# Another buffer pool for the last tile of a gated feed-forward result

## The chip, the cores and the metric

The kernel runs on one core of a Trainium2 chip. Its time is the device time of one launch, in microseconds (us); lower is better. Before the change it took 1318.67 us, the median of three runs (1316.35 to 1319.25). In what follows PE is the matrix engine, PEld its weight loads, DVE the vector engine, ACT the scalar engine, POOL the general engine, and SP the engine that issues most of the DMA transfers.

## The reference

Two layers work on 512 tokens of width 1024 in float32. Layer 0 mixes tokens by latent attention, layer 1 by a gated linear recurrence. Behind the mixer each layer does the same three steps:

```python
x = layer_norm(DEEPNORM_ALPHA * x + h, ln_mix_g[i], ln_mix_b[i])
x = layer_norm(DEEPNORM_ALPHA * x + swiglu_ffn(x, ffn_w_in[i], ffn_w_down[i]), ln_ffn_g[i], ln_ffn_b[i])
x = x + jax.nn.sigmoid(x @ ple_w_gate[i]) * (p[i] @ ple_w_proj[i])

def swiglu_ffn(x, w_in, w_down):
    h = x @ w_in
    g, u = h[..., :D_FF], h[..., D_FF:]
    return (jax.nn.silu(g) * u) @ w_down
```

The change lies in `swiglu_ffn`, once in each layer. D_FF is 2816, which is 22 blocks of 128.

## The kernel before, in words

**Number format.** A float32 product is made of three matmuls on split operands: each operand is a rounded high part and a low part (what is left), and `mm3` (lines 197 to 202) issues high x high, high x low and low x high. So every operand is split first: ACT copies the high part (line 179) and DVE subtracts it to get the low part (line 180). For weights of gate/up that come from memory, `split_dma` (lines 182 to 186) leaves the subtraction to a transfer: ACT writes the high part (184) and its negative (185), and POOL issues a transfer that adds the raw weights onto it (186).

**Gate/up** (`gate_up`, lines 380 to 476). One block j makes 128 columns of silu(g)·u for all 512 tokens. Blocks 0 and 1 are done plainly; blocks 2 to 21 use a Winograd scheme with seven products instead of eight. A product is four slices of the contraction, three matmuls each: 12 matmuls, so 84 per block. `prep(j)` loads the two weight blocks (SP, lines 391 and 392), forms the sums `ta` and `tb` on DVE (398 to 401), and splits: `h1`, `l1` and the pair `b22` with the help of POOL's transfers (395, 403), `h2`, `l2` from `ta` (405) and `h3`, `l3` from `tb` (407). `block(j)` then runs the products in the order A11·B11, A12·B21, S1·T1, S2·T2, A22·T4, S4·B22, S3·T3, and evacuates them with copies on ACT (439) and sums on DVE (446, 459 to 465). `b22` is first read by the sixth product, `h3` and `l3` by the fourth.

**The result** is kept in tiles of four blocks (`out`, lines 417 to 422). Five tiles of 8 KB per partition hold blocks 0 to 19; the last two blocks, 20 and 21, get a tile of 4 KB, [128, 2, 512] float32.

**The down projection** (`ffn`, lines 478 to 508) takes the 22 blocks one after the other. For each, SP loads 512 KB of down weights into a `raw` buffer, which are split into `whi` and `wlo` (`unit`, 188 to 195); `hsplit` (485 to 488) splits the block's result into a 4 KB `ma` tile; PE does 24 matmuls into eight banks.

**Buffers.** `mid` (171) hands out 4 KB buffers of two kinds, `ma` and `mb`, five of each (line 49). In gate/up each block takes three `ma` (`ta`, `tb`, `b22`) and two `mb` (`h3`, `l3`). There are five `whi`, five `wlo` and three `raw` buffers.

**The order.** A scheduler at compile time puts the instructions of each engine into one fixed queue, by the program's order and by when it expects operands and a free buffer. A tile whose buffer is not free there has its instructions put further back. On the chip each engine runs its queue strictly in order.

Of the kernel before, what the change touches and what calls it, by code (L numbers as in the profile page):

```python
# [29 lines left out]
P = 128  # L30
S = 512
# [114 lines left out]
class Builder:  # L146
# [233 lines left out]
    def gate_up(self, l, xT):  # L380
# [5 lines left out]
        hT = []  # L386
# [30 lines left out]
        def out(j):  # L417
            if j < 20 and j % 4 == 0:
                hT.append(self.slot([P, 4, S]))
            elif j == 20:  # L420
                hT.append(self.mid([P, 2, S]))
            return hT[j // 4][:, j % 4]

        def plain(h, w, half):
# [10 lines left out]
        def block(j):  # L435
            w = prep(j)
            h = out(j)
            part = lambda: self.small([P, N], tag="part", bufs=7)
            copy = lambda dst, src: nc.scalar.activation(dst, src[:, :N], AF.Copy)  # L439
# [26 lines left out]


        hs = [out(j) for j in range(2)]
        ws = [[self.unit(win[j, q], True) for q in range(2)] for j in range(2)]
        for half in range(2):  # L470
# [503 lines left out]
```

## Time and profile before

| | |
|---|---|
| time, median of 3 | 1318.67 us |
| profiled execution, its own time | 1319.56 us |
| its span, first to last instruction | 1317.8 us |
| PE busy | 1278.0 us (97%) |
| DVE busy | 813.1 us (62%) |
| ACT busy | 656.8 us (50%) |
| mean granted TensorE clock | 0.993 |

A span is measured between the first and the last instruction; the time of the execution includes the 1.76 us around it. PE is the engine with the least idle time, so the question is where PE waits, and on whom. The granted clock is the share of full speed at which PE was allowed to run. Tile names in the profile are those of the program without their numbers, so `ma` is any tile from the `ma` buffers.

### The profile page before, as it was taken

What the parts mean: (1) busy time and instruction counts of PE and PEld (TensorE: products, weight loads), DVE (VectorE), ACT (ScalarE), POOL (GpSimd) and SP (SyncE); (2) the same over time, 40 slices, a digit from 0 to 9 for tenths busy, and PEclk for the clock granted to TensorE, in tenths of its full rate; (3) what the DMA queues carried; (4) which work ended last, traced back from release to release, by engine and by line L of the source; (5) the groups of instructions that cost most, each with busy time, mean ns of one, the idle gap of its engine ahead of it and who ended that gap; (6) DMA issues with size and microseconds to landing.
All of it is one profiled execution on the core that took longest, in us unless ns stands there. A gap on an engine that the chain in (4) does not pass through costs nothing.

```text
span 1317.8 us, 20055 instructions
## 1 busy us (share of the span) xinstructions
PE 1278.0 (97%) x7900; PEld 1138.5 (86%) x7900; DVE 813.1 (62%) x1452; ACT 656.8 (50%) x1140; POOL 154.8 (12%) x167
## 2 busy tenths in 40 slices
PE   8999999999997999999999999999999999899998
PEld 8787889999997888888888887888999999688887
DVE  7998387777755333843377776459777774433473
ACT  6666267677654222633334344337776674422352
POOL 0200131111110000100002220023211110000000
PEclk9999999999998999999999999999999999899999
DMA  7213128778853333231412120314888873523321
GB/s 224 69 60 129 45 71 195 197 185 189 185 129 113 122 99 111 90 113 64 130 62 65 64 80 19 126 65 115 205 198 189 182 179 64 182 96 96 96 96 48
DMA packets 47614, 156.45 MB, mean 119 GB/s; under 512 B 5664, under 2 KB 5920, under 8 KB 47264
## 3 DMA queue, kind: packets, MB, share of 16 engines
q1 hardware_dynamic: 36000, 123.71, 29.1%
q0 software_dynamic: 11520, 31.46, 13.7%
q8 instruction: 62, 1.02, 0.3%
q14 instruction: 32, 0.26, 0.1%
HBM read 153.05 MB, written 2.10 MB: 118 GB/s over the span
## 4 chain that ended last, share of the span: by engine, by line
PE 83%; DVE 7%; DMA 5%; ACT 3%; issue 2%; POOL 1%; SPq 0%; DVEq 0%; ACTq 0%; POOLq 0%
PE ps L202 18%; PE ps L201 18%; PE ps L200 18%; PE sc L200 3%; PE sc L201 3%; PE sc L202 3%; DMA raw<-ffn_w_in 3%; PE wg L201 2%; PE wg L202 2%; PE wg L200 2%; PE tp L304 2%; PE sc L812 2%; PE tp L201 2%; PE tp L202 2%; PE tp L200 2%
## 5 line engine op out<-in xcount | busy, mean ns | idle before, releaser
L200 PE MATMUL ps<-big,whi 128*128 128x256 f32 (+1 forms) x768 | 237.0, 309 | 0.9 <-DVE part L459 0.9
L202 PE MATMUL ps<-big,wlo 128*128 128x256 f32 (+1 forms) x768 | 236.9, 308 | 0.2
L201 PE MATMUL ps<-big,whi 128*128 128x256 f32 (+1 forms) x768 | 235.5, 307 | 0.0
L180 DVE TENSOR_TENSOR wlo<-raw,whi 128x1024 fp32r<-128x1024 f32 (+1 forms) x123 | 148.2, 1209 | 82.6 <-ACT whi L179 80.9
L179 ACT ACTIVATE whi<-raw 128x1024 fp32r<-128x1024 f32 (+1 forms) x135 | 138.6, 1033 | 86.6 <-PE ps L202 35.5
L200 PE MATMUL ps<-whi,big 128*128 128x512 f32 (+2 forms) x440 | 170.7, 388 | 1.0 <-ACT big L179 1.0
L202 PE MATMUL ps<-whi,big 128*128 128x512 f32 (+2 forms) x440 | 168.2, 382 | 0.0
L201 PE MATMUL ps<-wlo,big 128*128 128x512 f32 (+2 forms) x440 | 168.0, 382 | 0.0
L200 PEld LDWEIGHTS ps<-big,whi 128*128 128x128 f32 x768 | 146.9, 191 | 5.9 <-DVE part L459 1.1
L202 PEld LDWEIGHTS ps<-big,wlo 128*128 128x128 f32 x768 | 146.8, 191 | 5.9 <-DVE wlo L180 0.6
L201 PEld LDWEIGHTS ps<-big,whi 128*128 128x128 f32 x768 | 146.8, 191 | 5.3
L200 PEld LDWEIGHTS ps<-whi,big 128*128 128x128 f32 x440 | 82.9, 188 | 15.4 <-ACT big L179 1.2
L202 PEld LDWEIGHTS ps<-whi,big 128*128 128x128 f32 x440 | 82.7, 188 | 15.5
L201 PEld LDWEIGHTS ps<-wlo,big 128*128 128x128 f32 x440 | 82.9, 189 | 14.5
L180 DVE TENSOR_TENSOR ma<-big,ma 128x512 fp32r<-128x512 f32 x40 | 27.5, 692 | 101.1 <-ACT ma L179 101.1
L179 ACT ACTIVATE ma<-big 128x512 fp32r<-128x512 f32 x40 | 25.0, 630 | 121.2 <-PE wg L202 121.0
L210 POOL TENSOR_TENSOR rr<-rv,mhalf 128x1 f32<-128x1 f32 (+2 forms) x28 | 26.6, 951 | 458.2 <-DVE rv L208 458.2
L180 DVE TENSOR_TENSOR wlo<-ma,whi 128x1024 fp32r<-128x1024 f32 x40 | 49.0, 1224 | 33.2 <-ACT whi L179 33.2
L186 POOL DMA_DIRECT2D ma<-ffn_w_in x40 | 34.8, 870 | 260.6 <-DVE big L460 130.2
L439 ACT ACTIVATE part<-ps 128x256 f32<-128x256 f32 x120 | 44.4, 373 | 41.9 <-PE ps L202 41.9
L201 PE MATMUL ps<-wlo,ma 128*128 128x512 f32 x164 | 64.2, 392 | 0.0
L202 PE MATMUL ps<-whi,ma 128*128 128x512 f32 x164 | 64.2, 392 | 0.0
(307 smaller groups left out, 3145.1 us busy)
## 6 DMA issues: line engine op xcount, KB each, us to landing
raw<-ffn_w_in SPq DMA_DIRECT2D x88, 512.0 KB, 4.7
raw<-ffn_w_down SPq DMA_DIRECT2D x44, 512.0 KB, 3.5
wlo<-ffn_w_in POOLq DMA_DIRECT2D x40, 512.0 KB, 6.9
ma<-ffn_w_in POOLq DMA_DIRECT2D x40, 256.0 KB, 6.8
raw<-ple_w_gate SPq DMA_DIRECT2D x16, 512.0 KB, 3.6
raw<-hgrn_w_fq SPq DMA_DIRECT2D x16, 512.0 KB, 3.5
raw<-mla_w_o SPq DMA_DIRECT2D x8, 512.0 KB, 3.6
raw<-hgrn_w_v SPq DMA_DIRECT2D x8, 512.0 KB, 4.4
```

Source lines behind the costliest of these rows:

```text
L179: self.nc.scalar.activation(hi, src, AF.Copy)
L180: (eng or self.nc.vector).tensor_tensor(out=lo, in0=src, in1=hi.bitcast(F32), op=ALU.subtract)
L186: self.nc.gpsimd.dma_start(lo, src, accum_op=ALU.add)
L200: mm(ps, a[0], b[0], start=start, stop=False, skip_group_check=more)
L201: mm(ps, a[0], b[1], start=False, stop=False, skip_group_check=more)
L202: mm(ps, a[1], b[0], start=False, stop=stop, skip_group_check=more)
L210: nc.gpsimd.tensor_tensor(out=r, in0=v, in1=self.mhalf[:, :n], op=ALU.pow)
L304: self.nc.tensor.transpose(out=ps[:, c * P:(c + 1) * P], in_=src[:, c * P:(c + 1) * P], identity=self.ident)
L439: copy = lambda dst, src: nc.scalar.activation(dst, src[:, :N], AF.Copy)
L812: nc.tensor.matmul(ps[:, c * P:(c + 1) * P], X[:, c * P:(c + 1) * P], pair_view(cs[0][:, :, 1, :], cs[1][:, :, 0, :]), start=True, stop=True)
```

## The change

The tile for blocks 20 and 21 comes from the `mb` buffers:

```diff
@@ -418,7 +418,7 @@
             if j < 20 and j % 4 == 0:
                 hT.append(self.slot([P, 4, S]))
             elif j == 20:
-                hT.append(self.mid([P, 2, S]))
+                hT.append(self.mid([P, 2, S], tag="mb"))
             return hT[j // 4][:, j % 4]
```

Both kinds of buffers have the same size, and no instruction is added or taken away. But the fixed queues come out in another order near the end of gate/up, in both layers alike. On DVE, at the place where blocks 18 and 19 of the first layer are evacuated (tiles `ma_4890` and `ma_4891` are `ta` and `tb` of block 21, `raw_4881` and `raw_4882` its weights, `wlo_4769` and `mb_4773` belong to block 20, and lines 446, 459 and 460 evacuate block 18):

```order
 L446 TENSOR_TENSOR part_4516<-sc_4515,part_4516 128x256
 L180 TENSOR_TENSOR wlo_4769<-ma_4758,whi_4768 128x1024
+L398 TENSOR_TENSOR ma_4890<-raw_4882 128x512
+L399 TENSOR_TENSOR ma_4890<-raw_4882,raw_4881 128x512
 L180 TENSOR_TENSOR mb_4773<-ma_4759,mb_4772 128x1024
+L400 TENSOR_TENSOR ma_4891<-ma_4890,raw_4881 128x512
 L459 TENSOR_TENSOR part_4545<-ps_4544,part_4545 128x256
+L401 TENSOR_TENSOR ma_4891<-ma_4891,raw_4881 128x512
 L460 TENSOR_TENSOR big_4251<-part_4545,part_4516 128x256
```

The four sums of block 21 now stand here, among the evacuations of block 18; before they stood two blocks further on, among those of block 20, the first of them behind line 460 of block 20.

On POOL, the transfers of blocks 20 and 21 (`ma_4896` is `b22` of block 21, `wlo_4886` the low part of its B11 and B21):

```order
 L186 DMA ma_4764<-ffn_w_in 128x512
 L186 DMA wlo_4754<-ffn_w_in 128x1024
+L186 DMA ma_4896<-ffn_w_in 128x512
 L186 DMA wlo_4886<-ffn_w_in 128x1024
-L186 DMA ma_4896<-ffn_w_in 128x512
 L210 TENSOR_TENSOR rr_5708<-rv_5706,mhalf 128x1
```

The transfer of `b22` now goes ahead of the other one of its block, as in block 20.

On ACT, with the change, from the last copy of block 19 to the `h3` of block 21 (`part_4717<-wg` is that copy; `part_4779`, `part_4809`, `part_4808` and `part_4849` belong to block 20; `ma_5066` and `ma_5099` are `hsplit` tiles of the down projection, `whi_5029` and `whi_5062` its weights 0 and 1, `mb_4904` is `h3` of block 21):

```order
L439 ACTIVATE part_4717<-wg_4704 128x256
L179 ACTIVATE ma_5066<-big_2124 128x512
L179 ACTIVATE whi_5029<-raw_5027 128x1024
L464 ACTIVATE part_4717<-part_4717 128x256
L439 ACTIVATE part_4779<-ps_4777 128x256
L179 ACTIVATE whi_5062<-raw_5060 128x1024
L447 ACTIVATE part_4779<-part_4779 128x256
L439 ACTIVATE part_4809<-ps_4807 128x256
L439 ACTIVATE part_4808<-ps_4777 128x256
L439 ACTIVATE part_4849<-wg_4836 128x256
L179 ACTIVATE ma_5099<-big_2124 128x512
L179 ACTIVATE mb_4904<-ma_4891 128x1024
```

Splits of the down projection stand between block 20's copies here. Before, none did: the queue had only the copies and lines 447 and 464 in this stretch, and the first split of the down projection stood behind the first copy of block 21.

## The prediction

> **What bounds the kernel now.** I read the page first, then the list of PE's own waits, then windows around the longest of them, then the single rows.
>
> ```profile
> PE 1278.0 (97%) x7900; PEld 1138.5 (86%) x7900; DVE 813.1 (62%) x1452; ACT 656.8 (50%) x1140; POOL 154.8 (12%) x167
> PEclk9999999999998999999999999999999999899999
> ```
>
> PE is busy nearly throughout, so a change off PE can only give what PE loses. The clock row shows two dips, in the slices from 395 to 428 us and from 1120 to 1153 us. PE's waits say what is there:
>
> ```profile
> PE ps L202 <- DMA ma<-ffn_w_in: 11.6, 2, 5.9
> PE ps L200 <- ACT mb L179: 1.5, 2, 0.7
> ```
>
> The largest wait in the program, 11.6 us in two pieces (one in each layer), is for a transfer into an `ma` tile from `ffn_w_in`: the low half of `b22` in `prep`. The second row also comes once a layer. Windows, with busy time and count for PE, PEld, DVE, ACT and POOL, then the granted clock, DMA share and GB/s:
>
> ```profile
> 394.20:404.20 10.00, 10.00 (x86) 10.00 (x85) 2.94 (x7) 2.38 (x6) 0.00 (x0) 1.00 0.01 2
> 404.00:424.00 20.00, 13.24 (x87) 12.58 (x86) 11.17 (x18) 9.74 (x17) 0.87 (x1) 0.74 0.51 171
> 424.00:537.00 113.00, 112.99 (x501) 93.23 (x501) 45.13 (x56) 34.45 (x45) 1.00 (x1) 1.00 0.34 107
> 1115.40:1135.40 20.00, 13.46 (x91) 12.67 (x90) 11.95 (x20) 10.18 (x18) 0.87 (x1) 0.83 0.51 172
> ```
>
> Just before 404 us PE does 86 matmuls in 10 us, with the DMA engines idle (0.01). Then 87 take 20 us. Behind that, the down projection runs with PE full for 113 us. So about 10 us a layer are lost in one place: block 21, the last of gate/up. The chain that ended last passes through there:
>
> ```profile
> 406.33 0.52 ACT ma L184
> 407.12 0.53 ACT ma L185
> 408.04 8.51 DMA ma<-ffn_w_in
> 416.59 0.58 PE ps L202
> ```
>
> **What block 21 costs today.** A block is seven products of 12 matmuls, 84 in all. In the first layer it begins at 404.01 and the down projection begins at 423.95; in the second, at 1115.49 and 1134.65:
>
> ```profile
> 404.01 0.28 PE L200 MATMUL ps<-big,whi 128*128 128x256 f32 x1
> ...
> 409.58 0.39 PE L200 MATMUL ps<-big,mb 128*128 128x256 f32 x1 [0.74 <-ACT mb L179]
> ...
> 410.39 0.28 PE L201 MATMUL ps<-big,ma 128*128 128x256 f32 x1
> 416.59 0.58 PE L202 MATMUL ps<-big,ma 128*128 128x256 f32 x1 [5.92 <-DMA ma<-ffn_w_in]
> ...
> 421.81 0.28 PE L201 MATMUL wg<-big,mb 128*128 128x256 f32 x1
> ...
> 423.95 0.40 PE L200 MATMUL tp<-whi,ma 128*128 128x512 f32 x1
> ```
>
> ```profile
> 1115.49 0.28 PE L200 MATMUL ps<-big,whi 128*128 128x256 f32 x1
> ...
> 1121.87 0.28 PE L201 MATMUL ps<-big,ma 128*128 128x256 f32 x1
> 1127.85 0.58 PE L202 MATMUL ps<-big,ma 128*128 128x256 f32 x1 [5.71 <-DMA ma<-ffn_w_in]
> ...
> 1131.79 0.28 PE L201 MATMUL wg<-big,mb 128*128 128x256 f32 x1
> ...
> 1134.65 0.40 PE L200 MATMUL tp<-whi,ma 128*128 128x512 f32 x1
> ```
>
> The undisturbed window shows 86 matmuls in 10.00 us, those counted that overlap its edges (each lasts 0.28): 10.28 / 86 = one start each 0.12 us. So a block is 84 x 0.12 = 10.08 us. Layer 0 takes 423.95 - 404.01 = 19.94, an excess of **9.86 us**; layer 1 takes 1134.65 - 1115.49 = 19.16, an excess of **9.08 us**. The excess of layer 0 splits so. The wait for the transfer, from start to start: 416.59 - 410.39 - 0.12 = 6.08. Behind it 24 steps to 421.81 take 5.22 instead of 2.88: 2.34 at the low clock, a start every 0.21. The wait for `mb`: about 0.90. The rest, small waits (for a `wlo` split and at handovers): 0.54. In layer 1: 5.86, then 18 steps in 3.94 instead of 2.16, which is 1.78, then 0.90 and 0.54.
>
> **Why the tile is late.** For block 20, DVE began to form the Winograd sums (line 398) at 369.54, ACT copied `b22` at 372.53 and POOL issued its accumulating transfer at 374.23. One block later, 10.08 us on, one expects 379.6, 382.6 and 384.3. What happened instead, on DVE and then on ACT:
>
> ```profile
> 369.54 0.69 DVE L398 TENSOR_TENSOR ma<-raw 128x512 f32<-128x512 f32 x1
> ...
> 402.84 0.42 DVE L459 TENSOR_TENSOR part<-ps,part 128x256 f32<-128x256 f32 x1 [5.34 <-PE ps L202]
> ...
> 403.64 0.68 DVE L398 TENSOR_TENSOR ma<-raw 128x512 f32<-128x512 f32 x1
> ...
> 404.84 0.42 DVE L462 TENSOR_TENSOR part<-ps,part 128x256 f32<-128x256 f32 x1
> ...
> 409.76 1.22 DVE L180 TENSOR_TENSOR mb<-ma,mb 128x1024 fp32r<-128x1024 f32 x1
> ```
>
> ```profile
> 372.53 0.63 ACT L184 ACTIVATE ma<-raw 128x512 fp32r<-128x512 f32 x1 [1.05 <-PE ps L202]
> ...
> 397.54 0.42 ACT L447 ACTIVATE part<-part 128x256 f32<-128x256 f32 x1 [1.58 <-DVE part L446]
> ...
> 401.33 0.39 ACT L439 ACTIVATE part<-wg 128x256 f32<-128x256 f32 x1 [0.99 <-PE wg L202]
> ...
> 406.23 0.61 ACT L184 ACTIVATE ma<-raw 128x512 fp32r<-128x512 f32 x1
> ...
> 408.49 1.04 ACT L179 ACTIVATE mb<-ma 128x1024 fp32r<-128x1024 f32 x1
> ...
> 410.00 0.62 ACT L179 ACTIVATE ma<-big 128x512 fp32r<-128x512 f32 x1
> ```
>
> POOL's and SP's own rows, and the median landing times in this stretch:
>
> ```profile
> 374.23 0.86 POOL L186 DMA_DIRECT2D ma<-ffn_w_in x1 [6.87 <-DVE big L460]
> 386.65 0.87 POOL L186 DMA_DIRECT2D wlo<-ffn_w_in  x1 [9.19 <-ACT part L439]
> 374.93 0.33 SPq L191 DMA_DIRECT2D raw<-ffn_w_down  x1
> 406.87 0.33 SPq L191 DMA_DIRECT2D raw<-ffn_w_down  x1
> ma<-ffn_w_in POOLq DMA_DIRECT2D x2, 256.0 KB, 7.6
> raw<-ffn_w_down SPq DMA_DIRECT2D x5, 512.0 KB, 6.2
> ```
>
> Line 398 came 24 us later than the rhythm, at a point where DVE had just idled 5.34 us. So DVE was not short of time: the instruction stands behind line 459 of block 20 in DVE's queue. The scheduler put it there because the tile of the last two blocks holds one of five `ma` buffers from block 20 on, which leaves four for the three of `prep(21)` and the three that block 20 still uses.
>
> **The change part by part.** No instruction is added or removed. With the tile in an `mb` buffer, the order shows lines 398 to 401 of block 21 back in the rhythm on DVE, and `b22`'s transfer first on POOL.
>
> *The transfer of `b22`.* Issued at about 384.3; landing takes 7.6 at the middle of the two in this window and 8.51 at the worst, so it is there by 393. Its product is the sixth, 60 matmuls into the block: 404.01 + 7.2 = 411.2. It is 18 us early. The wait of 6.08 and 5.86 goes, and with it the slow clock: 2.34 and 1.78. POOL's other transfer for block 21 (`wlo`) now goes second, one issue (0.86) later at most; it went out at 386.65 before and is first read by the third matmul, at 404.25, 17 us on.
>
> *The `mb` halves.* They are the tight step. On ACT the high half now stands behind the copy from `wg` (401.33 + 0.39) and one `hsplit` copy whose buffer is block 20's `b22`, free at 402.84 (the product that releases line 459). So: 402.84 + 0.62 + 1.04 = 404.5. On DVE the low half stands behind lines 462 and 463, which ended by 405.6 even with other work ahead of them; + 1.22 = 406.8. PE wants it with the 39th matmul of block 21: 404.01 + 38 x 0.12 = 408.6. That leaves 1.8 us, so the wait of 0.90 goes as well. Two `mb` buffers are free for it in time: four of five are held by blocks 19 and 20, block 18's second one goes to the result tile, and block 19's product in `wg` is over by about 391.3 (401.33 - 10.08), and with it the last read of its two.
>
> *The `wlo` of T1 and T3* now stands on DVE ahead of line 459 of block 19, so it is done by 392.8 (402.84 - 10.08), and PE reads it first in the third product, at 404.01 + 24 x 0.12 = 406.9. With that and the undisturbed run of the products the last 0.54 goes too.
>
> *What is added beside it.* Down weights 0 and 1, and their `h` halves, are now split inside blocks 19 and 20, in ACT's and DVE's idle time (2.38 and 2.94 busy in the last 10 us window). Raw buffers come free once `b22` has been copied, at 382.6 + 0.63, and the next load of down weights leaves then instead of at 406.87, so the loads of 512 KB move into a stretch where the DMA share was 0.01. The down projection ran without a wait of PE; it cannot become faster, only start earlier. The loads of the layer norm's parameters move behind three more loads on SP's queue; they are used at the end of the down projection, over 110 us later. In the rest of the program the order is unchanged.
>
> *Sum.* 9.86 + 9.08 = 18.94 us. The profiled execution took 1319.56 (span 1317.8 and 1.76 around it): 1300.6 is left. It lies 0.89 above the median of the runs shown, 1318.67, so against those the forecast is 1318.67 - 18.94 = **1299.7 us**. The terms' bounds: the transfer's and the clock's parts alone give 8.42 + 7.64 = 16.1 (1302.6); a clock term as large as layer 0's in both gives 19.5 (1299.2).
>
> The slow matmuls behind the wait (24 and 18 of them) vary between the layers. [...]
>
> **The rivals.**
>
> *A. The wait moves to the `mb` halves.* For it: the slack is 1.8 us, on two queues that have taken on other work, and PE did wait here before (0.74). Against it: everything ahead of them is counted. If the low half is 4 us late against my walk, PE loses 2.2 a layer: 1299.7 + 4.4 = 1304.1; with a slow clock on top, 2 x (2.2 + 2.34) = 9.1, or 1308.8.
>
> *B. Slower: down weights in front of block 20's copies on ACT.* The split of down weight 1 now stands ahead of lines 447 and 439 of block 20, in order. It needs that load, issued at about 383.3. If the load came after 401.1 - 1.04 - 0.42 - 0.39 = 399.2 (PE needs line 439's copy for the sixth product of block 20, which began at 404.01 - 10.08 = 393.93: 393.93 + 7.2), PE would stand still, us for us. To lose more than the 9.5 gained a layer it would have to take 25.4 us; at 28 us the time is 1318.7 + 2 x (2.6 + 2.3) = 1328. Against it: such loads land in 6.2, and the DMA engines are nearly idle.
>
> *C. Nothing gained.* PE's start of the down projection is earlier, but the end of the layer is set by something else: 1318.7. Against it: PE is full for 112.99 of 113 us behind it. Or the scheduler's order turns out not to hold the buffer early: the order rows speak against it.
>
> **How the numbers follow.** The forecast 0.83, A 0.10, B 0.04, C 0.03. The forecast's own range is 1297 to 1303: bounds of the terms, and the runs of before that reach from 1316.35 to 1319.25. Up to 1306 takes in the milder half of A. A measurement of this kernel can tell about 0.2% (2.6 us) from no change. Faster: 0.83 + 0.10 = 0.93; same: C, 0.03; slower: B, 0.04.
>
> **What would show it.** PE's list of waits has no row for `ma<-ffn_w_in`, and none for `mb` behind ACT line 179; windows of 20 us that begin with block 21 hold PE busy at clock 1.00; the page's clock row has no dip in the two slices. Line 398 of block 21 runs near 380 us, POOL's second `ma` transfer near 384, the down projection begins near 414.1, and in layer 1 near 1115.5 - 9.9 + 10.1 = 1115.7. Wrong would be: a PE wait of over 1 us in blocks 19 to 21 for `mb`, or for a copy of line 439 behind a down weight on ACT; or a down projection that begins at 414 but ends where it did.

## The result and the profile after

The changed kernel takes 1299.09 us, the median of four runs (1297.99 to 1300.91), against 1318.2 us before (four runs, 1316.35 to 1319.25). The ratio is 0.9858, with a 95% interval of 0.9841 to 0.9875: 19.1 us less by the medians, where 1299.7 us was forecast. One execution among the experiments below was disturbed as a whole (3235 us) and is left out; that kernel was run a second time for its profile.

The page of the kernel after, its span, busy times and clock row:

```profile
span 1297.0 us, 20093 instructions
PE 1272.0 (98%) x7900; PEld 1134.2 (87%) x7900; DVE 809.7 (62%) x1452; ACT 658.5 (51%) x1140; POOL 154.7 (12%) x167
PEclk9999999999999999999999999999999999999999
```

The span is 20.8 us shorter (1317.8 - 1297.0). PE's busy time is 6.0 us shorter too, though it does the same 7900 matmuls. Of this, 4.1 us are the steps at the low clock (2.34 and 1.78), which count as busy for longer; both dips of the clock row are gone. PE's own waits after, the longest and the one for `mb` (engine, operation and line, who released it, then us in total, times, longest):

```profile
PE tp L200 <- ACT whi L179: 5.2, 1, 5.2
PE tp L304 <- DVE big L344: 4.7, 4, 1.3
PE ps L200 <- ACT part L439: 3.0, 5, 1.0
...
PE wg L201 <- DVE mb L180: 0.9, 1, 0.9
```

The list's rows for `ma<-ffn_w_in` (11.6 us before) are gone, and so is `mb` behind ACT line 179 (1.5 us before). The last row stands in both lists with 0.9. Nothing that is left lies in block 21. Windows with the columns of those before (length, busy time and count of PE, PEld, DVE, ACT and POOL, granted clock, DMA share, GB/s):

```profile
394.20:404.20 10.00, 10.00 (x86) 10.00 (x85) 5.25 (x10) 5.51 (x11) 0.00 (x0) 1.00 0.35 107
404.00:424.00 20.00, 20.00 (x128) 18.22 (x128) 10.75 (x17) 8.35 (x14) 0.00 (x0) 1.00 0.42 150
```

Between 404 and 424 us PE now is busy for all 20.00 us (13.24 before) at clock 1.00 (0.74 before). In the ten microseconds ahead of it, DVE and ACT do about twice the work that they did (5.25 and 5.51 us; 2.94 and 2.38 before), and the DMA engines, idle there before, run at 0.35. Block 21 on PE, its first product and the first of the down projection behind it, layer 0 and then layer 1:

```profile
403.59 0.28 PE L200 MATMUL ps<-big,whi 128*128 128x256 f32 x1
...
413.67 0.40 PE L200 MATMUL tp<-whi,ma 128*128 128x512 f32 x1
...
1103.88 0.28 PE L200 MATMUL ps<-big,whi 128*128 128x256 f32 x1
...
1113.96 0.40 PE L200 MATMUL tp<-whi,ma 128*128 128x512 f32 x1
```

Both blocks take 10.08 us (413.67 - 403.59 and 1113.96 - 1103.88), which is 84 products at 0.12, where they took 19.94 and 19.16. The preparation of block 21 on DVE, ACT and POOL, and then the step that the prediction called tight, its two `mb` halves:

```profile
379.20 0.69 DVE L398 TENSOR_TENSOR ma<-raw 128x512 f32<-128x512 f32 x1
...
382.19 0.63 ACT L184 ACTIVATE ma<-raw 128x512 fp32r<-128x512 f32 x1 [1.05 <-PE ps L202]
...
383.89 0.87 POOL L186 DMA_DIRECT2D ma<-ffn_w_in  x1 [6.85 <-DVE big L460]
386.23 0.87 POOL L186 DMA_DIRECT2D wlo<-ffn_w_in  x1 [1.47 <-ACT part L439]
...
402.89 1.04 ACT L179 ACTIVATE mb<-ma 128x1024 fp32r<-128x1024 f32 x1
...
404.49 1.22 DVE L180 TENSOR_TENSOR mb<-ma,mb 128x1024 fp32r<-128x1024 f32 x1
```

Line 398 starts at 379.20 instead of 403.64, the transfer of `b22` is issued at 383.89 instead of 408.04, and the low half of T2 and T4 is done at 405.71; the product that reads it starts at 403.59 + 38 x 0.12 = 408.15.

### The profile page after: what moved, and what is told of

It reads as the page before. It is cut to its first block, busy times and chain, and to the rows that moved or that the text cites. A ratio compares the mean times of both kernels' runs of the same rounds, so it can differ in the third digit from the quotient of the medians.

```text
span 1297.0 us, 20093 instructions
## 1 busy us (share of the span) xinstructions
PE 1272.0 (98%) x7900; PEld 1134.2 (87%) x7900; DVE 809.7 (62%) x1452; ACT 658.5 (51%) x1140; POOL 154.7 (12%) x167
## 4 chain that ended last, share of the span: by engine, by line
PE 83%; DVE 7%; DMA 4%; ACT 3%; issue 2%; POOL 1%; SPq 0%; DVEq 0%; ACTq 0%; POOLq 0%
PE ps L200 18%; PE ps L201 18%; PE ps L202 18%; PE sc L200 3%; DMA raw<-ffn_w_in 3%; PE sc L201 3%; PE sc L202 3%; PE wg L201 2%; PE wg L200 2%; PE wg L202 2%; PE tp L304 2%; PE sc L812 2%; PE tp L201 2%; PE tp L202 2%; PE tp L200 2%
## 5 line engine op out<-in xcount | busy, mean ns | idle before, releaser
L202 PE MATMUL ps<-whi,ma 128*128 128x512 f32 x164 | 64.2, 392 | 0.0
L200 PE MATMUL ps<-whi,ma 128*128 128x512 f32 x164 | 64.0, 390 | 0.0
L180 DVE TENSOR_TENSOR mb<-ma,mb 128x1024 fp32r<-128x1024 f32 x40 | 48.9, 1222 | 6.3 <-ACT mb L179 3.4
```

The source lines that it names most:

```text
L180: (eng or self.nc.vector).tensor_tensor(out=lo, in0=src, in1=hi.bitcast(F32), op=ALU.subtract)
L200: mm(ps, a[0], b[0], start=start, stop=False, skip_group_check=more)
L202: mm(ps, a[1], b[0], start=False, stop=stop, skip_group_check=more)
```

## Experiments

**Theories.** T: the loss came from the place of block 21's lines 398 to 401 in DVE's fixed queue, and PE paid for it through one transfer that was issued late (plus the slow clock behind the idle time). Rivals: the kind of buffer, or the number of free `ma` buffers, matters at run time; the late preparation costs in itself, transfer or not; the wait is only hidden by some slack in `mb` that could be used up; the half rate (a granted clock of 0.50, and a start every 0.21 us in place of 0.12) has nothing to do with PE's idling.

**1. The tile stays in `ma`, the preparation is written earlier.**

```diff
         def block(j):
-            w = prep(j)
+            w = ahead.pop(j) if j in ahead else prep(j)
+            if j == 20:
+                ahead[21] = prep(21)
             h = out(j)
...
+        ahead = {}
         hs = [out(j) for j in range(2)]
```

> The kernel before, its result tile still in a buffer of kind ma, but the weight preparation of block 21 is written in the program ahead of block 20's request for that tile, so that the three ma tiles of block 21 are handed out first and the result tile gets the buffer that comes after them. Theory (the loss is the place of block 21's lines 398 to 401 in DVE's fixed queue, behind line 460 of block 20, and that place follows from the turn in which the ma buffers are handed out): line 398 of block 21 starts near 380 us in layer 0, the transfer into the second block-22 half starts near 384 us, no wait of the products for it, and the time is that of the change, 1299 us (1297 to 1302). Rival (the tile must be off the ma buffers, because four that are left cannot feed two blocks at once, whatever the order): the wait for the transfer stays at 4 us or more in each layer and the time stays at 1310 to 1319 us.

Measured: 1300.1 us (1299.76 to 1300.4), ratio to the kernel before 0.9859 (0.9842 to 0.9875), the same as the change within the intervals. On DVE and POOL of this kernel:

```profile
379.46 0.69 DVE L398 TENSOR_TENSOR ma<-raw 128x512 f32<-128x512 f32 x1
...
384.15 0.86 POOL L186 DMA_DIRECT2D ma<-ffn_w_in  x1 [6.85 <-DVE big L462]
```

So the tile need not be off the `ma` buffers. What counts is the order in the program, from which the queues are made: block 21's whole preparation now asks for its buffers first, and the tile after it.

**2. The change in mb, with line 398 held back.** The opposite test: the tile is in `mb`, and one tiny copy makes line 398 wait for line 460 of block 20.

```diff
             lo, up = slice(0, 512), slice(512, 1024)
+            if j == NF - 1:
+                v.tensor_copy(ta[:, 512:513], hT[-1][:, 0, 0:1])
             v.tensor_tensor(out=ta[:, up], in0=rb[:, up], in1=rb[:, lo], op=ALU.subtract)
...
-                hT.append(self.mid([P, 2, S]))
+                hT.append(self.mid([P, 2, S], tag="mb"))
```

> The kernel after the change, the result tile in mb, with one instruction more in block 21 of each layer: one column of block 20's result is copied into block 21's first ma tile ahead of line 398, so that line 398 has to stand behind line 460 of block 20 again (the column is overwritten by line 398). In the fixed order this puts DVE's rows back to where they were before the change, and TensorE's as well. Theory (the place in DVE's queue is enough, whatever kind the tile is of): line 398 of block 21 starts at 403.6 us in layer 0, the products wait 5 to 6 us for the transfer in each layer, the time is that of before, 1318 us (1315.5 to 1320). Rival (with five ma buffers free the later preparation is caught up, or the kind of buffer itself matters at run time): 1312 us or less, the wait for the transfer under 3 us.

Measured: 1318.27 us (ten runs, 1315.78 to 1319.55), ratio 1.0002 (0.9992 to 1.0012). The whole gain is gone. DVE, where line 400 is what was line 398 and line 462 what was 460, and then PE and its waits:

```profile
403.16 0.43 DVE L462 TENSOR_TENSOR mb<-part,part 128x256 f32<-128x256 f32 x1
403.62 0.15 DVE L399 COPY ma<-mb 128x1 f32<-128x1 f32 x1
403.81 0.69 DVE L400 TENSOR_TENSOR ma<-raw 128x512 f32<-128x512 f32 x1
```

```profile
415.75 0.58 PE L202 MATMUL ps<-big,ma 128*128 128x256 f32 x1 [5.52 <-DMA ma<-ffn_w_in]
...
1125.87 0.58 PE L202 MATMUL ps<-big,ma 128*128 128x256 f32 x1 [5.60 <-DMA ma<-ffn_w_in]
```

With experiment 1 this settles the cause: an early place of line 398 in DVE's queue goes with the gain without the other buffer, and a late place alone takes the gain away with the other buffer.

**3. The change in layer 0 alone.**

```diff
-                hT.append(self.mid([P, 2, S], tag="mb"))
+                hT.append(self.mid([P, 2, S], tag="mb" if l == 0 else "ma"))
```

> The change in layer 0 alone; layer 1 takes the tile from ma as before. Theory (each layer loses its own wait, 9.86 us in layer 0 and 9.08 us in layer 1, and neither depends on the other): 1318.2 - 9.9 = 1308.3 us (1306.5 to 1310.5), block 21 of layer 0 takes 10.08 us of products and block 21 of layer 1 still about 19.2 us with the wait of 5.7 us for the transfer. Rival (the 1.8 us by which the change gained more than the two blocks' excess belong to one layer's start, or layer 0's gain is given back in layer 1): off 1308.3 us by 2 us or more, with the two blocks as said.

Measured: 1308.06 us (1306.98 to 1308.87), ratio 0.9918 (0.9903 to 0.9932). Layer 1 alone still shows its two waits, 0.75 and 5.43 us:

```profile
1108.87 0.38 PE L200 MATMUL ps<-big,mb 128*128 128x256 f32 x1 [0.75 <-ACT mb L179]
1115.38 0.58 PE L202 MATMUL ps<-big,ma 128*128 128x256 f32 x1 [5.43 <-DMA ma<-ffn_w_in]
```

The gain is the sum of two halves: against the 1318.2 us beside the change, 10.1 us in layer 0 and 9.0 more in layer 1 (to 1299.09), against 9.86 and 9.08 in the sum. The runs of the kernel before that belong to this experiment have a median of 1319.07 us, which would make it 11.0 in layer 0; so the halves are known to a microsecond or two.

**4. The transfer taken away, the preparation left late.** The kernel before, with the low half of `b22` in block 21 made by DVE:

```diff
-            self.split_dma(b22[:, 0], b22[:, 1], rb[:, up], win[j, 1][:, up])
+            if j == NF - 1:
+                self.split(b22[:, 0], b22[:, 1], rb[:, up].rearrange("p (a b) -> p a b", a=1)[:, 0])
+            else:
+                self.split_dma(b22[:, 0], b22[:, 1], rb[:, up], win[j, 1][:, up])
```

> The kernel before, but in block 21 of each layer the low half of the twice-used weight part B22 is made by a subtraction on DVE, like the other splits, in place of POOL's accumulating transfer; the preparation stays as late as before, behind line 460 of block 20. Theory (the late preparation costs little by itself; what PE pays for is the transfer issued late, 6.08 and 5.86 us, and the slow clock behind it, 2.34 and 1.78 us): both go, the waits for mb halves of 0.74 us or so stay or double since the subtractions on DVE stand in one row: 1318.2 - 16.1 = 1302 us (1300 to 1306). Rival (any late preparation costs about as much, since DVE's four subtractions and the splits are themselves too late for the products): PE waits 3 us or more for mb or ma halves per layer, 1308 to 1316 us.

> The kernel of the run with the split by a subtraction once more, for a profile of an ordinary execution: in that run's time the preparation cost nothing although it stays late. Theory (what counts is the transfer alone, and the order of the products that the planner chose because of it): line 398 of block 21 near 403.6 us, the low halves of T2 ready no later than the products reach them, no wait above 1 us in block 21, 84 products in 10.1 to 10.8 us. Rival (something else sped up): waits of 1 us or more stay in block 21 and another stretch is shorter than in the kernel after the change. 1299.5 us (1298 to 1301) by the first run's times.

Measured: 1299.33 us in the first run (median of three executions, 1298.4 to 1299.79), ratio 0.9851 (0.9834 to 0.9867), and 1299.57 us in the second, of one execution. That is about 2.5 us better than expected, and as good as the change. DVE and then PE in block 21 of the second run:

```profile
403.02 0.68 DVE L398 TENSOR_TENSOR ma<-raw 128x512 f32<-128x512 f32 x1
...
407.56 0.68 DVE L180 TENSOR_TENSOR ma<-raw,ma 128x512 fp32r<-128x512 f32 x1
...
409.63 1.22 DVE L180 TENSOR_TENSOR mb<-ma,mb 128x1024 fp32r<-128x1024 f32 x1
```

```profile
408.05 0.70 PE L200 MATMUL tp<-whi,ma 128*128 128x512 f32 x2
...
409.78 0.28 PE L200 MATMUL ps<-big,ma 128*128 128x256 f32 x1
...
411.22 0.28 PE L202 MATMUL ps<-big,mb 128*128 128x256 f32 x1
```

The preparation is as late as in the kernel before (403.02), yet PE's list of waits has none of block 21. `b22`'s low half is there at 408.24, and not at 416.6. The low half of T2 comes at 410.85; the planner, which knew of it, put five products of the down projection (operands `whi,ma`, from 408.05 on) and the twelve of B22 (409.78 to 411.10) in front of the first product that reads it, at 411.22. That is why the 0.9 us for `mb`, which I had left in this run's expectation, went too. So the rival "late is dear in itself" is wrong here: the late preparation cost only through the transfer's time from issue to landing, and through the order of the products around it.

**5. One `mb` buffer less.** The kernel after, with one more `mb` tile held from block 20's request to the end of block 21:

```diff
             elif j == 20:
                 hT.append(self.mid([P, 2, S], tag="mb"))
+                held.append(self.mid([P, 2, S], tag="mb"))
+                v.memset(held[0][:, 0, 0:1], 0.0)
...
+            if j == NF - 1:
+                v.tensor_copy(held[0][:, 0, 0:1], h[:, N:N + 1])
```

> The kernel after the change, with one more tile of kind mb taken with the result tile and held until the end of block 21 (one column of it is written at the start and at the end, two tiny instructions on DVE), so that three mb buffers in place of four are left for the split halves T2 and T4 of blocks 20 and 21. Theory (the mb halves of block 21 have slack: the low half is done 2.4 us before the product that reads it): the low half now has to wait until block 20's last product from its mb halves is through, about 3 us ahead of block 21's start, and is still in time; 1299 to 1300.5 us. Rival A of the prediction (the wait moves to the mb halves once buffers run short): a wait of PE for mb of 2 to 5 us in block 21 of each layer, with the slow clock behind it 1304 to 1309 us.

Measured: 1299.96 us (1298.92 to 1301.47), ratio 0.9858 (0.9843 to 0.9872). The two halves:

```profile
402.85 1.04 ACT L179 ACTIVATE mb<-ma 128x1024 fp32r<-128x1024 f32 x1
...
404.45 1.22 DVE L180 TENSOR_TENSOR mb<-ma,mb 128x1024 fp32r<-128x1024 f32 x1
```

They come at the same times as without the held tile (402.89 and 404.49). The number of free `mb` buffers is not what sets these times, and one less costs nothing here. Rival A has neither its wait nor its condition.

**6. PE kept busy while it waits.** The kernel before, with products added ahead of the one that waits; their result is read by nobody:

```diff
             copy(g1, d)
+            if j == NF - 1:
+                idle = self.bank("tp")
+                for k in range(44):
+                    nc.tensor.matmul(idle[:, :N], w["B22"][0][:, k % 4 * P:(k % 4 + 1) * P], xT("S4")[0][:, k % 4],
+                                     start=True, stop=True)
             product(C, xT("S4"), w["B22"], True)
```

> The kernel before, with 44 products of 128x256 more in block 21 of each layer, into a PSUM bank that nobody reads, from data that are there early: the fixed order puts 18 of them between the products of S1 and S2 and 26 right ahead of the product that waits for the transfer, and has the other products of the block in front of the wait, so that 24 are left behind it. PE then stays busy until the transfer lands (416.6 us in layer 0). Theory (the half rate of 24 and 18 steps comes from PE's idle time): all steps at 0.12 us, block 21 of layer 0 ends at 419.5 to 420.5 us in place of 423.95, about 3.8 us per layer, 1311.5 us (1309.5 to 1313.5). Rival (the half rate comes from the transfer or the time, not from idling): 24 steps at 0.21 us, 2.3 us later per layer, 1316 us (1314.5 to 1318).

> As the run with the wait filled, but 22 further products in place of 44: 18 as there, 4 right ahead of the wait, so that PE is done near 414.5 us in layer 0 and idles about 2.1 us until the transfer lands at 416.6 us. Theory A (an idle time as short as that leaves the clock alone, as the 0.74 us gap does in the kernel before): 24 steps at 0.12 us behind it, end at 419.5 us, 1310.5 us (1309 to 1312.5). Theory B (any idle time above about 1 us halves the rate): 24 steps at 0.21 us, 421.7 us, 1315 us (1313 to 1317).

Measured: 1310.94 us with 44 products (1310.41 to 1312.54; ratio 0.995, 0.9934 to 0.9966) and 1311.68 us with 22 (1309.55 to 1314.87; ratio 0.9952, 0.9937 to 0.9967). PE with 44:

```profile
413.79 3.28 PE L461 MATMUL tp<-big,ma 128*128 128x256 f32 x26
416.91 0.28 PE L200 MATMUL ps<-big,ma 128*128 128x256 f32 x1
...
419.67 0.28 PE L202 MATMUL ps<-big,wlo 128*128 128x256 f32 x1
419.79 0.40 PE L200 MATMUL tp<-whi,ma 128*128 128x512 f32 x1
```

The 24 products behind the transfer take 419.79 - 416.91 = 2.88 us, 0.12 each, and the granted clock is 1.00 from 404 to 420 us, though the transfer was issued as late as ever (408.18; 408.04 in the kernel before). So the half rate here comes from PE's idling, and neither from the transfer nor from the place in the program. In layer 0 the down projection starts 4.16 us earlier than before the change (419.79 against 423.95): 2.34 of that is the clock, and the rest is there because the planner now has all other products of the block in front of the wait. What stays of the loss is the late landing. With 22 the waits were 1.79 and 2.73 us, and the products behind both kept 0.12 (the second wait as PE shows it):

```profile
1124.15 0.39 PE L202 MATMUL ps<-big,ma 128*128 128x256 f32 x1 [2.73 <-DMA ma<-ffn_w_in]
```

That is theory A for the profiled execution. The others of the same kernel differ, though: the two fastest (1309.55 and 1309.75 us) show a mean granted clock of 1.000, the slowest (1314.87) 0.997. The next two were to find from which length of wait on the half rate comes; they differ from the run with 22 by their 20 added products of 128 columns, shown here, or of 64:

```diff
-                for k in range(22):
-                    nc.tensor.matmul(idle[:, :N], w["B22"][0][:, k % 4 * P:(k % 4 + 1) * P], xT("S4")[0][:, k % 4],
+                for k in range(20):
+                    nc.tensor.matmul(idle[:, :128], w["B22"][0][:, k % 4 * P:(k % 4 + 1) * P], xT("S4")[0][:, k % 4, :128],
                                      start=True, stop=True)
```

> As the run with the short gap, but 20 further products that read 128 columns in place of 22 that read 256; the other products stand in the same order. If such a product takes 0.06 us in place of 0.12, PE comes 1.2 to 1.4 us earlier to the wait and idles about 3.1 us in layer 0 and 4.0 us in layer 1 (1.79 and 2.73 us in the run with the short gap). Open so far: between a gap of 2.73 us, behind which the steps were 0.12 us, and one of 5.43 us, behind which they were 0.21 us, where the half rate begins. Theory A (a bound at an idle time of some 3.4 us): 0.12 us behind 3.1 us, 0.21 us behind 4.0 us; 1312 us. Theory B (a bound nearer 5 us): 0.12 us behind both, 1310.5 us. Theory C (a bound nearer 2.8 us): 0.21 us behind both, 1315 us.

> As the run before it, with 20 further products that read 64 columns: if such a product takes 0.03 us, PE idles about 4.0 us in layer 0 and 4.9 us in layer 1 before the transfer lands. Theory A: 0.21 us per step behind both gaps, for 18 to 24 steps, 1314.5 us. Theory B: 0.12 us behind the gap of 4.0 us, 0.21 us behind that of 4.9 us or 0.12 us behind both, 1310.5 to 1312.5 us. If the 64-column products take as long as the 128-column ones (the weight load sets their rate), the gaps are those of the run before it and so is the result.

Measured, one execution each: 1312.1 and 1311.43 us. The gaps aimed at were missed: they are 1.14 and 2.14 us with 128 columns, 1.96 and 2.79 us with 64. In a run of narrower products the starts are 0.11 us apart, hardly less than 0.12, and with 128 columns the planner put ten of them right ahead of the wait, where it had put four with 256 (and two with 64). But what followed the waits fits none of the three theories. With 128 columns, layer 1:

```profile
1123.02 0.39 PE L202 MATMUL ps<-big,ma 128*128 128x256 f32 x1 [2.14 <-DMA ma<-ffn_w_in]
1123.24 0.28 PE L200 MATMUL ps<-big,ma 128*128 128x256 f32 x1
...
1124.07 0.40 PE L201 MATMUL ps<-big,ma 128*128 128x256 f32 x1
1124.27 0.41 PE L202 MATMUL ps<-big,ma 128*128 128x256 f32 x1
```

With 64 columns, layer 0, and then layer 1:

```profile
416.14 0.58 PE L202 MATMUL ps<-big,ma 128*128 128x256 f32 x1 [1.96 <-DMA ma<-ffn_w_in]
416.52 0.41 PE L200 MATMUL ps<-big,ma 128*128 128x256 f32 x1
...
1123.84 0.39 PE L202 MATMUL ps<-big,ma 128*128 128x256 f32 x1 [2.79 <-DMA ma<-ffn_w_in]
1124.06 0.28 PE L200 MATMUL ps<-big,ma 128*128 128x256 f32 x1
```

Waits of 1.96 and 2.14 us were followed by a stretch at half rate, waits of 2.73 and 2.79 us were not. The length of the wait alone does not decide.

## Why the prediction was right, point by point

**The sum.** It was 18.94 us; the medians show 19.1 and the two profiled spans 20.8. Block 21 gave exactly its two terms: 19.94 - 10.08 = 9.86 and 19.16 - 10.08 = 9.08. What the spans show beyond that, 1.9 us, lies outside block 21 (its start in layer 0 came 0.42 us earlier, 403.59 against 404.01, ahead of anything that the change moves). About 1.0 us more of it arises early in gate/up of layer 1: PE's waits there come to 2.13 us before (0.89 and 1.24, ending at 944.76 and 947.70) and to 1.07 after (0.36 and 0.71, ending at 927.88 and 936.04). In experiment 2, which has block 21's late order, they come to 1.21 us, and its profiled span is 1316.6 us, 1.2 us off the 1317.8 of the kernel before. So most of the 1.9 us is scatter between executions, and not part of the change (the medians differ by 19.1 only).

**The walk.** Line 398, ACT's copy, POOL's transfer: forecast 379.6, 382.6, 384.3, measured 379.20, 382.19, 383.89, each 0.4 earlier, as block 21 itself is. The start of the down projection was forecast at 414.1 and 1115.7, measured at 413.67 and 1113.96; the second is 1.7 us off, since block 21 of layer 1 began at 1103.88 and not at 1115.49 - 9.86 = 1105.63; that is the same remainder as in the spans. The other transfer on POOL (`wlo`) went out second at 386.23, as said.

**The `mb` halves.** The high half was done at 403.93 (forecast 404.5), the low half at 405.71 (406.8). The slack was 2.44 us, not 1.8, and experiment 5 shows that it does not hang on free buffers either.

**Rival B** (down weights ahead of block 20's copies on ACT) had its condition in the queue, but not its price. The load was there long before (issued at 382.85, it landed 3.5 us later):

```profile
396.47 1.06 ACT L179 ACTIVATE whi<-raw 128x1024 fp32r<-128x1024 f32 x1 [0.93 <-PE sc L201]
397.43 0.40 ACT L447 ACTIVATE part<-part 128x256 f32<-128x256 f32 x1
```

ACT's idle time ahead of the split of down weight 1 ended with a product of PE, and line 447 followed 0.96 us later. PE has no wait for line 439's copies in block 20. **Rival C** fell with the 19.1 us.

**Why the tile is late: half right.** The prediction's place was right (line 398 behind line 460 in DVE's queue; experiment 2 reproduces the old time from it). Its reason, that the tile leaves only four `ma` buffers for six users, does not explain the 24 us. In the kernel before, `ta` and `tb` of block 20 were split by 382.3, and the last product that reads block 19's `b22` is this one:

```profile
392.37 0.28 PE L202 MATMUL ps<-big,ma 128*128 128x256 f32 x1
```

From 392.65 on, then, block 20's `b22` and at most the result tile hold an `ma` buffer, so three of five are free. Line 398 needs one and DVE idles, yet it starts at 403.64 only. (Experiment 1 does not test the count, since there the tile is asked for behind block 21's three.) What the rows show instead is that line 398, whose buffer is asked for behind the result tile and from the same kind, stands right behind line 460 of block 20, the first to write that tile (403.64 and 403.30). With the change the tile's kind is `mb`, and there the high `mb` half starts with line 460, at 402.89 and 402.88, though it is on ACT's queue:

```profile
402.88 0.42 DVE L460 TENSOR_TENSOR mb<-part,part 128x256 f32<-128x256 f32 x1
```

In experiment 1, where the tile is not in `mb`, the high half comes at 386.26. So it looks as if the planner serves the requests of one kind in their order, and the tile's only when its first writer is due. One row speaks against it (in experiment 5 the held tile, asked for behind the result tile, is written at 381.77 already), so the rule by which the planner hands out buffers stays open. It would explain why the `mb` halves come so late with the change, but they have 2.4 us to spare, and no transfer behind them.

**The clock.** The terms 2.34 and 1.78 us were right as sizes of what happened, and experiment 6 shows that they came from PE's idling. (The starts went from 0.12 to 0.21 us apart, which is 1.8 times, while the granted clock halved, from 1.00 to 0.50.) A shorter wait cost its own length only in the runs with 1.14, 1.79, 2.73 and 2.79 us, but not in those with 1.96 and 2.14. There some 15 steps at 0.21 in place of 0.12 added about 1.4 us. In the kernel before, the clock fell 0.80 us into the wait in layer 0 and 2.71 us into the one in layer 1, as the last section shows.

## What to carry to other kernels

When one transfer in a steady rhythm goes out late, look at what stands in front of its first instruction in the engine's fixed queue: a tile that is asked for in the midst of a ring of buffers can push the next block's preparation back by two blocks, and moving that one request to another pool, or behind the preparation in the program, are equal cures. Price a late preparation by its longest step, which here was the transfer (8.5 and 8.3 us from issue to landing in the two layers of the kernel before); a step on an engine that comes just as late may cost nothing, if the planner has other products to put ahead (experiment 4, 1299.33 us). And where PE is otherwise full, a stall can cost more than its length: here the waits of 5.92 and 5.71 us brought 2.34 and 1.78 us more at half rate.

## What the runs showed of the hardware beyond the forecast

In these runs the half rate behind a wait is not set by the length of the wait alone. In the six short waits for the transfer, 1.14, 1.79, 2.73 and 2.79 us were followed by starts every 0.12 us, and 1.96 and 2.14 us by starts every 0.21. In the case of 2.14 us the half rate did not begin with the first product after the wait, but 1.05 us later (1123.02 to 1124.07); in the case of 1.96 us it was on from the first. Behind the long waits (5.43 to 5.92 us) it was on from the first each time.

Nor does the clock fall at a fixed distance from PE's last product. In the kernel before, it fell 0.80 us behind that product's end in layer 0 (410.67 and 411.47) and 2.71 us behind it in layer 1 (1122.15 and 1124.86), and was 0.50 for 10.24 and 6.83 us. In layer 1 of the run with 128 columns it fell at 1124.07 and was 0.50 for 3.41 us. Here are windows, with their length, PE's busy time and count, granted clock, DMA share and GB/s, three of the kernel before and three of the run with 128 columns, and then two of the run with 22 products of 256, which show the other engines too:

```profile
408.05:411.47 3.42, 1.87 (x13) 1.00 0.85 327
411.47:421.71 10.24, 5.12 (x24) 0.50 0.66 220
1124.86:1131.69 6.83, 3.84 (x18) 0.50 0.70 244
...
1120.66:1124.07 3.41, 1.27 (x10) 1.00 0.93 348
1124.07:1127.48 3.41, 3.41 (x18) 0.50 0.38 117
1127.48:1130.89 3.41, 3.41 (x16) 1.00 0.71 207
```

```profile
1120.28:1123.69 3.41, 1.14 (x10) 0.93 (x8) 0.65 (x2) 0.39 (x1) 0.00 (x0) 1.00 1.06 338
1111.00:1127.00 16.00, 13.27 (x108) 12.90 (x107) 11.17 (x17) 10.85 (x18) 0.87 (x1) 1.00 0.63 215
```

PE's busy time does not decide alone either. In layer 0 of the kernel before PE was busy for 1.87 of the 3.42 us ahead of the fall, which also hold the wait of 0.74 us for `mb`; in the run with 128 columns for 1.27 of 3.41 us. But with 22 products of 256 columns PE was busy for 1.14 of the 3.41 us that hold most of its wait of 2.73 us, and the clock was 1.00 from 1111 to 1127. The clock came back while PE was at work: in the kernel before 5.12 us after the start of the first product behind the wait in layer 0 (416.59 to 421.71) and 3.84 us after it in layer 1 (1127.85 to 1131.69). What sets the fall and the return stays open, and so does the spread of the run with 22 products (1309.55 to 1314.87 us, clock 1.000 to 0.997).

Further, products of 64 and 128 columns here start hardly faster than those of 256: inside a run of them 0.11 us apart, against 0.12, with a weight load each (nine of 64 columns take 1.08 us and two take 0.31, so each further one 0.11). So narrower products hardly shortened a stretch of them.
